# Conditioning products on VectorE, float32r biases and gates before the combine in a two-block diffusion transformer on one core

## The chip, the cores and the metric

The kernel runs on one NeuronCore of a Trainium2 chip. TensorE (PE) multiplies matrices into PSUM, VectorE (DVE) and ScalarE (ACT) work on SBUF and PSUM, GpSimd (POOL) helps, and SyncE (SP) issues nearly all DMA transfers of weights. The metric is device time in microseconds (us), the median of several runs. A profiled execution gives a span and a trace; its own time is a little longer than its span.

## What is computed

A batch of one: 256 tokens and 256 context tokens of width 1024 go through two transformer blocks, all in float32. Cut to what matters here:

```python
silu_c = jax.nn.silu(c)                                   # block 1; block 2 has its own c_2
mod = split(silu_c @ w_mod + b_mod, 6)                    # 6 vectors of 1024, from a 1024 x 6144 matrix
h = rmsnorm(x, norm_mix_g) * (1 + mod[1]) + mod[0]
x = x + mod[2] * token_mixer(h, h_ctx, ...)               # HGRN2 scans, latent attention, projections
h = rmsnorm(x, norm_ffn_g) * (1 + mod[4]) + mod[3]
x = x + mod[5] * moe_ffn(h, ...)                          # 32 experts, 4 for each token
    # per expert: gu = xb @ w_gate_up[e] + b_gate_up[e];  act = glu(gu);  y = act @ w_down[e] + b_down[e]
x = rmsnorm(x, final_norm_g)
x = second_block(x, c_2, ...)   # silu(c_2) @ w_ada + b_ada, RWKV7 and RG-LRU branches, a MoE of 4 x 8 experts
shf, scf = split(silu(c_2) @ w_ada_f + b_ada_f, 2)        # final norm: rmsnorm(x) * (1 + scf) + shf
```

The vectors `mod`, their counterparts of block 2 and `shf`, `scf` are called conditioning vectors below. The first 2048 columns of `w_mod` are needed at once and computed at the start by `mod_first`, which the change leaves alone.

## The kernel before

There are four stages: block 1 (0 to 576 us), its MoE (to 1540), block 2 (to 1842) and its MoE (to 2109).

**The queue of block 1.** Work on TensorE comes as Items: `prep` requests weights (1 MB tiles in a ring of five buffers), `run` is a generator that issues the products. `step` (L451) runs the first Item of the queue and prepares the first two, so weights are requested two Items ahead. Between the pieces of the HGRN2 scans, `fill` takes Items from the queue. A projection Item splits its weights in two float32r parts, `wsh` on ScalarE (L495) and the remainder `wsl` on VectorE (L496), and multiplies three times (L508 to L510, tile `tp`). All engines run their instructions in the order in which the program issues them.

**Conditioning products.** `mod(which, j)` (L371) is an Item with two 1 MB tiles: 512 of the outputs as a row, from 8 float32 products per tile pair (`modrow`, L367, into `modps`), added into the table `rowall` on VectorE (L369). `cpad` holds the silu of the conditioning so that a product writes one row. The list `MODS1` has 20 of them; `mixed` puts one behind each projection Item of block 1. The last four (`wadaf`) are loaded and run at the start of block 2. `mod_cols` later turns rows into columns, and `bcast_rows` (L425) broadcasts a row over all partitions by one product of 512 columns.

**The MoE of block 1** (`moe1`, `expert1a`, `expert1b`). For each expert 12 tiles of 1 MB come in. `expert1a` multiplies the 64 gathered tokens' columns with 8 of them into `gu` (L1327; two 64-row halves, two column halves), adds the bias by four products of 32 x 64 with rows of `brows` (L1402), and VectorE and ScalarE make the activation. `expert1b`, delayed by one expert, multiplies with the other four into `y` (L1358) and adds two bias products. `combine` (L1240) splits `y` times the slot weight into `yhi` (ScalarE, L1236) and `ylo` (VectorE, L1237), scatters with products `co` (L1248), and on VectorE four times multiplies by the gate vector (`gated`, L1253) and adds into `x` (L1254). Every four experts, tokens are gathered anew (`ga`, L1278). After expert 11 (`OVF`) the pending down product runs at once, expert 12's weights are requested into named buffers, and a branch for overfull experts is read (L1292).

**The start of block 2.** The four `wadaf` Items are put in the queue, two of them loaded ahead, then one tile of the projection weights. x is normalised (`xh`, L1672 and L1682), transposed on TensorE (`xT`, L1710), mixed (`hp`, `xm`), and projected.

Of the kernel before, what the change touches and what calls it, by code (L numbers as in the profile page):

```python
# [23 lines left out]
MODS1 = [(1, j) for j in range(4, 12)] + [(2, j) for j in range(12)]  # L24
NWS, NU, NV = 8, 32, 20
NWR = 5
# [5 lines left out]
def _cols(a):  # L32
# [23 lines left out]
def _khalf(w):  # L56

    t = w.shape[1] // 512
    return np.ascontiguousarray(w.reshape(2, 4, 128, t, 512).transpose(3, 0, 2, 1, 4)).reshape(2 * t, 128, 2048)
# [62 lines left out]
def layout(i):  # L122
# [12 lines left out]
    d['wmod'] = _khalf(i['w_mod'][0])  # L135
    d['wmix'] = _ktile(i['w_mod'][0][:, :2048])
    d['wada'] = _khalf(i['w_ada_2'][0])
    d['wadaf'] = _khalf(i['w_ada_f_2'])
    mix = i['b_mod'][0][:2048].reshape(2, 4, 256).transpose(1, 0, 2).reshape(-1)
    d['bmods'] = np.ascontiguousarray(np.concatenate([mix, i['b_mod'][0][2048:], i['b_ada_2'][0], i['b_ada_f_2'], mix]).reshape(32, 512))  # L140
# [36 lines left out]
class Item:  # L177

    def __init__(self, prep, run):
        self.prep, self.run = prep, run  # L180
        self.ready = self.done = False
        self.gen = self.then = None
# [57 lines left out]
class Ker:  # L240
    def __init__(self, tc, d, out, dbg=None, stop=None, start=1):
        self.tc, self.nc, self.d, self.out = tc, tc.nc, d, out
        self.dbg = dbg or {}
        self.stop, self.start = stop, start
# [5 lines left out]
    def run(self):  # L250
        with ExitStack() as es:
# [10 lines left out]
            if self.start <= 1:  # L262
                with tc.tile_pool(name="t1late", bufs=1, side="right") as pl, tc.tile_pool(name="t1", bufs=1) as p:
                    self.early = lambda n: p.tile([128, 512], F32, name=n, tag="u", bufs=NU)
                    self.consts()
                    route = self.block1(p, pl, xtile)
            else:
                self.early = lambda n: self.cp.tile([128, 512], F32, name=n)
                self.consts()
                self.x1 = xtile("x").rearrange("p a (b n) -> p (a b n)", b=1).rearrange("p (b n) -> p b n", b=2)  # L270
                self.nc.sync.dma_start(self.x1, self.d['xin'])
                self.add(*(self.mod(2, j) for j in range(12)))
                self.drain()
                self.mod_cols((12, 10, self.mcol2[:, 0:40]))
# [4 lines left out]
            if self.start > 1:  # L279
                self.load_gf()  # L280
            if self.start <= 1:
                with tc.tile_pool(name="moe1", bufs=1, side="right", reuse_waits="tile") as p, tc.tile_pool(name="w2", bufs=NW2, reuse_waits="tile") as wp2, tc.tile_pool(name="w2x", bufs=NW2X, reuse_waits="tile") as wp3:
                    self.wq = own * NWR + [(wp3, "w")] * NW2X + [(wp2, "w")] * NW2
                    self.moe1(p, route, (wp2, "w"), (wp3, "w"))
# [29 lines left out]
    def consts(self):  # L314
# [23 lines left out]
        self.cpad2 = cp.tile([128, 504], F32, name="cpad2").rearrange("p (k n) -> p k n", k=8)  # L338
        nc.gpsimd.memset(self.cpad2, 0.0)
        nc.gpsimd.tensor_copy(self.cpad2[:, :, 31], cs[:, 16:24])  # L340
# [6 lines left out]
        self.mcol2 = cp.tile([128, 48], F32, name="mcol2")  # L347

# [4 lines left out]
    def msrc(self, which, j):  # L353
        src, r = {1: ('wmod', j), 2: ('wada', 12 + j), 3: ('wadaf', 24 + j)}[which]
        return [self.d[src][2 * j + a] for a in range(2)], r
# [57 lines left out]
    def mod_cols(self, *todo):  # L413

        pt = self.fold_rows()
        for r, n, dst in todo:
            self.nc.vector.tensor_copy(dst.rearrange("p (j g) -> p g j", g=4), pt.rearrange("p (g r) -> p g r", g=4)[:, :, r:r + n])

    def bcast_rows(self, keys, dst, last=None):

        nc = self.nc
        for key, o in zip(keys, dst):
            ps = self.ps("bc")
            r = self.msrc(*key)[1]
            nc.tensor.matmul(ps, self.fold[:, r:r + 1].to_broadcast([128, 128]), self.rowall, start=True, stop=True)  # L425
            (last or nc.scalar.copy)(o, ps)
# [8 lines left out]
    def add(self, *items):  # L435
        self.q += items
        return items[-1]
# [99 lines left out]
    def block1(self, p, late, xtile):  # L537
# [255 lines left out]

        mods = [self.mod(*m) for m in MODS1]
        def mixed(items):
            out = []
            for it in items:
                out.append(it)
                if mods:
                    out.append(mods.pop(0))  # L800
# [66 lines left out]
        for pr in range(4):  # L867
# [4 lines left out]
            else:  # L872
                nxt = None
                lnexp()
                for i in range(3):
                    self.later(4 * i, lambda i=i: readout(i))
                self.add(*(tproj(win[28 + a], LAT, keep(qa, "qa", 3, qnorm)) for a in range(3)),
                         tproj(win[31], HS, keep(ckv, "ckv", 2, cnorm)), tproj(d['wrope'], HS, keep(kr, "kr"), nb=1, n=1024))
# [1352 lines left out]
```

## Time and profile before

| | us |
|---|---|
| runs, median (lowest to highest of 3) | 2112.69 (2109.07 to 2114.51) |
| the profiled execution, own time | 2111.07 |
| its span | 2109.3 |
| TensorE busy, in the span | 1945.5 (92%) |
| VectorE busy | 896.0 (42%) |
| ScalarE busy | 511.6 (24%) |

Busy shares are means over four stages with different limits, so the table by stretch and the slices of the span say more than they do. Matmuls are pipelined, and a busy TensorE is not one at its peak. A wait is put down to what came last; idle time of an engine that does not set the end costs nothing.

### The profile page before, as it was taken

How to read it: one execution, taken by the hardware profiler on the slowest of the kernel's cores; microseconds unless marked ns; L12 is line 12 of the kernel's file. 1: busy time of each engine (PE TensorE's matmuls, PEld its weight loads, DVE VectorE, ACT ScalarE, POOL GpSimd, SP SyncE). 2: the span in 40 equal slices, each digit the busy share in tenths (PEclk: the TensorE clock that was granted, in tenths of full speed). 3: DMA queues.
4: the chain of work that ended last, by engine and by line, in shares of the span. 5: the costliest groups of instructions: out<-in, count | busy, mean ns of one | idle time of the engine just before them, and what ended most of it. 6: DMA issues, size and time to landing. Idle time of an engine off the chain costs nothing. (4 is left out here: it accounts for less than half of the span.)

```text
span 2109.3 us, 30791 instructions
## 1 busy us (share of the span) xinstructions
PE 1945.5 (92%) x12860; PEld 1114.6 (53%) x12861; DVE 896.0 (42%) x1727; ACT 511.6 (24%) x893; POOL 63.3 (3%) x66
## 2 busy tenths in 40 slices
PE   5999999999899999989999999999969998899785
PEld 3888788877733333333333333333338997764331
DVE  5666754445423233332323333242378574421112
ACT  3433454344300001000000100000035543311011
POOL 0000000000000000000000000000032201000000
PEclk9999999999999999989999999999989999989897
DMA  9255636732699999979999999999873133289895
GB/s 362 81 219 201 227 126 258 278 111 80 262 415 427 411 427 416 427 295 407 426 427 427 426 427 427 426 427 427 365 292 124 62 121 103 114 370 420 360 425 226
DMA packets 95272, 646.11 MB, mean 306 GB/s; under 512 B 11668, under 2 KB 12692, under 8 KB 19220
## 3 DMA queue, kind: packets, MB, share of 16 engines
q1 hardware_dynamic: 93296, 642.79, 74.9%
q8 instruction: 104, 1.70, 0.3%
q10 hardware_dynamic: 1828, 1.26, 0.2%
q14 instruction: 44, 0.36, 0.0%
HBM read 642.96 MB, written 1.05 MB: 305 GB/s over the span
## 5 line engine op out<-in xcount | busy, mean ns | idle before, releaser
L1327 PE MATMUL gu<-w,gT 128*64 128x512 f32 x2048 | 481.2, 597 | 0.0
L1327 PEld LDWEIGHTS gu<-w,gT 128*64 128x64 f32 x2048 | 148.1, 137 | 278.1 <-issue 263.1
L1358 PE MATMUL y<-w,aT 128*64 128x512 f32 x1024 | 229.4, 601 | 0.4
L496 DVE TENSOR_TENSOR wsl<-w,wsh 128x1024 fp32r<-128x1024 f32 (+1 forms) x141 | 168.6, 1205 | 97.6 <-ACT wsh L495 97.3
L495 ACT CAST wsh<-w 128x1024 fp32r<-128x1024 f32 (+1 forms) x141 | 143.4, 1030 | 169.0 <-PE tp L509 97.4
L1337 DVE TENSOR_SCALAR act<-gu 128x256 f32<-128x256 f32 x64 | 27.2, 425 | 307.5 <-PE gu L1402 304.2
L1237 DVE SCALAR_TENSOR_TENSOR ylo<-y,sw,yhi 128x512 fp32r<-128x512 f32 x52 | 39.0, 751 | 264.5 <-ACT yhi L1236 264.0
L1358 PEld LDWEIGHTS y<-w,aT 128*64 128x64 f32 x1024 | 71.9, 139 | 148.6 <-issue 143.7
L508 PE MATMUL tp<-hs,wsh 128*128 128x256 f32 (+1 forms) x424 | 139.7, 329 | 0.0
L510 PE MATMUL tp<-hs,wsl 128*128 128x256 f32 (+1 forms) x424 | 134.3, 317 | 4.1 <-DVE wsl L496 4.1
L509 PE MATMUL tp<-hs,wsh 128*128 128x256 f32 (+1 forms) x424 | 133.6, 315 | 0.0
L1529 PE MATMUL ab<-w,gT 128*32 128x256 f32 (+1 forms) x1024 | 99.8, 415 | 17.4 <-DMA w<-in_w1e_dram 10.8
L1236 ACT ACTIVATE yhi<-y,sw 128x512 fp32r<-128x512 f32 x52 | 35.8, 688 | 300.9 <-PE y L1402 239.9
L1253 DVE TENSOR_TENSOR gated<-co,gtb 128x512 f32<-128x512 f32 x128 | 88.3, 690 | 34.6 <-PE co L1248 27.5
L1339 ACT ACTIVATE sge<-act 128x512 f32<-128x512 f32 x32 | 20.1, 630 | 331.3 <-DVE act L1337 331.3
L508 PEld LDWEIGHTS tp<-hs,wsh 128*128 128x128 f32 x424 | 81.7, 193 | 16.3 <-issue 4.9
L1254 DVE TENSOR_TENSOR x<-x,gated 128x512 f32<-128x512 f32 x128 | 88.3, 690 | 3.3
L510 PEld LDWEIGHTS tp<-hs,wsl 128*128 128x128 f32 x424 | 81.6, 193 | 9.9 <-DVE wsl L496 4.9
L508 PE MATMUL tp<-hi,wsh 128*128 128x256 f32 x288 | 85.4, 296 | 0.0
L509 PEld LDWEIGHTS tp<-hs,wsh 128*128 128x128 f32 x424 | 81.8, 193 | 4.5 <-issue 0.7
L1278 PE MATMUL ga<-oh,xhi 128*128 128x256 f32 x208 | 63.5, 333 | 21.9 <-PEq L1292 6.3
L509 PE MATMUL tp<-lo,wsh 128*128 128x256 f32 x288 | 81.7, 284 | 0.0
(576 smaller groups left out, 3099.9 us busy)
## 6 DMA issues: line engine op xcount, KB each, us to landing
w<-in_wgu_dram SPq DMA_DIRECT2D x256, 1024.0 KB, 15.3
w<-in_wdn_dram SPq DMA_DIRECT2D x128, 1024.0 KB, 15.6
w<-in_win_dram SPq DMA_DIRECT2D x50, 1024.0 KB, 5.9
w<-in_w3e_dram SPq DMA_DIRECT2D x32, 1024.0 KB, 14.7
w<-in_w1e_dram SPq DMA_DIRECT2D x32, 1024.0 KB, 11.9
w<-in_w2e_dram SPq DMA_DIRECT2D x32, 1024.0 KB, 15.9
w<-in_wada_dram SPq DMA_DIRECT2D x24, 1024.0 KB, 6.4
w<-in_wmod_dram SPq DMA_DIRECT2D x16, 1024.0 KB, 6.0
```

The costliest lines, as they stand in the source:

```text
L495: nc.scalar.copy(hi, src)
L496: nc.vector.tensor_sub(lo, src, hi.bitcast(F32))
L508: nc.tensor.matmul(out, a[0], b[0], start=first, stop=False)
L509: nc.tensor.matmul(out, a[0], b[1], start=False, stop=False)
L510: nc.tensor.matmul(out, a[1], b[0], start=False, stop=last)
L1237: nc.vector.scalar_tensor_tensor(lo, y, w, hi.bitcast(F32), op0=OP.mult, op1=OP.subtract)
L1253: nc.vector.tensor_mul(part, o[s], gate[:, cs])
L1254: nc.vector.tensor_add(x[:, b, cs], x[:, b, cs], part)
L1278: nc.tensor.matmul(ps[:, 256 * kk:256 * kk + 64 * n], xs[i][:, b, 128 * (k + kk):128 * (k + kk) + 128], ohv[b], start=(b + i == 0), stop=( ...
L1327: nc.tensor.matmul(gu[j][64 * s:64 * s + 64, :], g[:, k, c0:c0 + 64], w[:, 1024 * s + 512 * j:1024 * s + 512 * j + 512], start=(k == 0), s ...
L1358: nc.tensor.matmul(y[64 * s:64 * s + 64, :], aT[:, k % 4, k // 4, :], w[:, o:o + 512], start=(k == 0), stop=False)
L1529: nc.tensor.matmul(ps[m * j:m * j + m, 256 * i:256 * i + 256], g[:, k, c0 + m * j:c0 + m * j + m], w[j][:, k, :], start=(k == 0), stop=(k ...
```

## The change

**Conditioning products on VectorE.** The host transposes `w_mod`, `w_ada` and `w_ada_f` so that outputs lie on partitions. `crow` broadcasts the silu of the conditioning over 128 partitions (eight products and two copies, once for c and once for c_2). An Item is now half a former one, with one 1 MB tile and two `scalar_tensor_tensor` instructions of 128x1024 with an accumulator; a bias add of 128x2 follows. The result is a column of `mcol1`, `mcol2` or `mcol3`. Halves are `light`: `step` prepares them when it meets them and counts only other Items to two. All 24, the four `wadaf` too, run in block 1: one half behind each projection of the scans, one behind each of the latent projections, two behind the gates `g7` and the query projections, the rest behind the last key/value Item.

**Biases.** Bias rows are split once into float32r parts, high and low on 64 partitions for each half, and an expert adds them with one selection matrix (`brow`, made on VectorE, 128x128) and three products: two into `gu`, one into `y`.

**Gates.** `expert1b` multiplies `y` by the gate once (128x512) before the split; `combine` then adds `co` from PSUM into `x` directly.

**Block 2** starts without conditioning products; its first projection tile is requested first.

```diff
-MODS1 = [(1, j) for j in range(4, 12)] + [(2, j) for j in range(12)]
+MODS = [(1, j) for j in range(4, 12)] + [(2, j) for j in range(12)] + [(3, j) for j in range(4)]
...
     def step(self):
         it = self.q[0]
-        for i in self.q[:2]:
+        n = 0
+        for i in self.q:
             if not i.ready:
                 i.ready, i.w = True, i.prep()
+            n += not i.light
+            if n == 2:
+                break
...
-    def mod(self, which, j):
-        src, r = self.msrc(which, j)
-        cpad = self.cpad1 if which == 1 else self.cpad2
-        def run(ws):
-            yield from self.modrow(cpad, r, [(0, lambda k: ws[k // 4][:, 512 * (k % 4):512 * (k % 4) + 512])])
-        return Item(lambda: [self.wload(t) for t in src], run)
+    def mod(self, p, which, j):
...
+        def half(a):
+            def run(w):
+                yield 0
...
+                for i in range(2):
+                    wi = w[:, 1024 * i:1024 * i + 1024]
+                    n = 2 * a + i
+                    nc.vector.scalar_tensor_tensor(wi, wi, 1.0, c, op0=OP.mult, op1=OP.mult, accum_out=o[:, n:n + 1])
+                o = o[:, 2 * a:2 * a + 2]
+                b = VOFF[bias] + 4 * j + 2 * a
+                nc.vector.tensor_add(o, o, self.vec[:, b:b + 2])
+            return Item(lambda: self.wload(self.d[src][2 * j + a]), run, True)
+        return [half(0), half(1)]
...
-        lastg = [self.add(tproj(win[24 + i], LAT, g7)) for i in range(4)][-1]
+        lastg = [self.add(*mixed([tproj(win[24 + i], LAT, g7)], 2)) for i in range(4)][-1]
...
         for j in range(2):
-            for s in range(2):
-                bias(gu[j][64 * s:64 * s + 64, :], 0, 1024 * s + 512 * j)
+            bias(gu[j], 0, 512 * j)
...
-        for s in range(2):
-            bias(y[64 * s:64 * s + 64, :], 1, 512 * s)
-        self.combine(p, x, y, oT, wv, gate)
+        bias(y, 1, 0)
+        part = p.tile([128, 512], F32, name="gated", tag="gated", bufs=1)
+        nc.vector.tensor_mul(part, y, gate)
+        self.combine(p, x, part, oT, wv)
...
-        mods = [self.mod(3, j) for j in range(4)]
-        self.add(*mods)
-        for m in mods[:2]:
-            m.ready, m.w = True, m.prep()
         ahead = [(self.wload(win2[2]),)]
```

What this moves on VectorE shows in block 1 between the latent keys and the softmax. Before, around the gate projections (`wsl` is a projection's weight remainder, `sg` and `s` the gate's sigmoid, `rowall` the add of a conditioning product):

```order
L369 TENSOR_TENSOR rowall<-rowall,modps 128x512
L496 TENSOR_TENSOR wsl<-w,wsh 128x1024 x2
L864 TENSOR_TENSOR sg<-sg,tp 128x512
L865 TENSOR_TENSOR s_3680<-s_3680,sg 128x512
L369 TENSOR_TENSOR rowall<-rowall,modps 128x512
L496 TENSOR_TENSOR wsl<-w,wsh 128x1024 x9
L496 TENSOR_TENSOR wsl<-w,wsh 128x512
L496 TENSOR_TENSOR wsl<-w,wsh 128x1024
```

And now, in the same place, around the projections of `g7` and the queries (`mcol` is a conditioning column, `crow` the broadcast silu):

```order
L507 TENSOR_TENSOR wsl<-w,wsh 128x1024 x2
L386 SCALAR_TENSOR_TENSOR w,mcol_97<-w,crow 128x1024 x2
L389 TENSOR_TENSOR mcol_97<-mcol_97,vec 128x2
L386 SCALAR_TENSOR_TENSOR w,mcol_97<-w,crow 128x1024 x2
L389 TENSOR_TENSOR mcol_97<-mcol_97,vec 128x2
L507 TENSOR_TENSOR wsl<-w,wsh 128x1024 x2
L386 SCALAR_TENSOR_TENSOR w,mcol_97<-w,crow 128x1024 x2
L389 TENSOR_TENSOR mcol_97<-mcol_97,vec 128x2
L386 SCALAR_TENSOR_TENSOR w,mcol_97<-w,crow 128x1024 x2
L389 TENSOR_TENSOR mcol_97<-mcol_97,vec 128x2
L507 TENSOR_TENSOR wsl<-w,wsh 128x1024
L507 TENSOR_TENSOR wsl<-w,wsh 128x512
```

Four full-width instructions stand between one Item's remainders and the next one's, where one add stood or none. From the latent keys' normalisation to the ninth softmax reduction the order has 64 of them; in front of it 32: 14 up to the first scan pair's readout copy, 11 in the second pair, 7 in the third.

In the MoE of block 1, VectorE's instructions behind an expert's down product were:

```order
L1237 SCALAR_TENSOR_TENSOR ylo<-y,sw,yhi 128x512
L1253 TENSOR_TENSOR gated<-co,gtb_5348 128x512
L1254 TENSOR_TENSOR x<-x,gated 128x512
L1253 TENSOR_TENSOR gated<-co,gtb_5348 128x512
L1254 TENSOR_TENSOR x<-x,gated 128x512
L1253 TENSOR_TENSOR gated<-co,gtb_5348 128x512
L1254 TENSOR_TENSOR x<-x,gated 128x512
L1253 TENSOR_TENSOR gated<-co,gtb_5348 128x512
L1264 CAST oT<-wT 128x256
L1254 TENSOR_TENSOR x<-x,gated 128x512
```

They are now (`blk` and `fc` make the selection matrix of the next bias):

```order
L1376 TENSOR_TENSOR gated<-y,gtb_5348 128x512
L1438 TENSOR_SCALAR brow<-blk,fc 128x128
L1251 SCALAR_TENSOR_TENSOR ylo<-gated,sw,yhi 128x512
L1270 TENSOR_TENSOR x<-x,co 128x512 x4
L1280 CAST oT<-wT 128x256
```

One product by the gate stands before the split instead of four behind the scatter.

## Rows read from the trace of the kernel before

**Rows 1.** The page: span, busy time of engines, and GB/s in 40 slices.

```profile
span 2109.3 us, 30791 instructions
...
PE 1945.5 (92%) x12860; PEld 1114.6 (53%) x12861; DVE 896.0 (42%) x1727; ACT 511.6 (24%) x893; POOL 63.3 (3%) x66
...
GB/s 362 81 219 201 227 126 258 278 111 80 262 415 427 411 427 416 427 295 407 426 427 427 426 427 427 426 427 427 365 292 124 62 121 103 114 370 420 360 425 226
```

**Rows 2.** Stretches: from:to, length, busy us (instructions) by engine, clock, DMA share, GB/s.

```profile
64.00:143.00 79.00, 75.50 (x504) 64.67 (x503) 56.91 (x135) 34.92 (x71) 0.00 (x0) 0.96 0.47 174
143.00:211.00 68.00, 68.00 (x469) 56.65 (x468) 39.95 (x99) 26.91 (x58) 0.00 (x0) 1.00 0.49 186
211.00:271.00 60.00, 60.00 (x403) 48.61 (x402) 39.38 (x99) 26.05 (x58) 0.00 (x0) 1.00 0.57 211
...
322.00:489.00 167.00, 162.02 (x1152) 130.72 (x1150) 78.78 (x116) 69.13 (x104) 0.00 (x0) 1.00 0.58 211
...
950.00:1400.00 450.00, 438.58 (x2196) 154.92 (x2193) 147.28 (x261) 35.72 (x58) 0.00 (x0) 1.00 1.01 424
1537.00:1570.00 33.00, 17.23 (x109) 7.54 (x109) 25.63 (x39) 13.12 (x26) 14.15 (x16) 0.74 0.77 292
```

**Rows 3.** Stretches, instructions on the tile modps alone: PE, PEld, DVE busy.

```profile
64.00:143.00 79.00, 5.98 (x48) 1.15 (x48) 2.05 (x3) 0.96 0.47 174
143.00:211.00 68.00, 7.90 (x64) 1.57 (x64) 2.73 (x4) 1.00 0.49 186
...
322.00:425.00 103.00, 15.39 (x128) 3.34 (x128) 5.47 (x8) 1.00 0.73 273
```

**Rows 4.** Groups by line, VectorE, 64 to 322: count, busy us, mean ns.

```profile
L369 DVE TENSOR_TENSOR rowall<-rowall,modps 128x512 f32<-128x512 f32 x12 | 8.2, 684 | 2.0 <-PE modps L367 1.9
...
L680 DVE MEMSET ex<- 128x1 f32 x7 | 0.4, 59 | 0.0
```

**Rows 5.** Two lines, whole trace: duration ns min/median/max, first and last start.

```profile
L1138 DVE SCALAR_TENSOR_TENSOR xlo<-x,rs,xhi x4: 1276/1278/1279, 569.1 to 1838.7; 128x1024 fp32r<-128x1024 f32 x4
...
L957 ACT ACTIVATION_READ_ACCUMULATOR pr<-sc,st x16: 191/192/195, 440.2 to 523.3; 128x1 f32 x16
```

**Rows 6.** Groups by line, VectorE, 1537 to 1570: busy us, mean ns.

```profile
L1253 DVE TENSOR_TENSOR gated<-co,gtb 128x512 f32<-128x512 f32 x4 | 2.8, 690 | 0.7 <-PE co L1248 0.6
...
L1237 DVE SCALAR_TENSOR_TENSOR ylo<-y,sw,yhi 128x512 fp32r<-128x512 f32 x1 | 0.8, 751 | 6.6 <-ACT yhi L1236 6.6
L1676 DVE SCALAR_TENSOR_TENSOR tn<-tn,tn 128x1 f32<-128x1 f32 x2 | 0.3, 155 | 0.1
```

**Rows 7.** TensorE's waits, 322 to 489: us in total, times, longest.

```profile
PE tp L510 <- DVE wsl L496: 4.1, 3, 1.6
```

**Rows 8.** Timeline after expert 11: start, us, engine, instruction [idle before <-releaser].

```profile
905.50 1.93 PE L1402 MATMUL gu<-brows,fc 32*64 32x512 f32 x8
...
914.38 1.07 PE L1402 MATMUL y<-brows,fc 32*64 32x512 f32 x4
...
939.68 0.55 PE L1278 MATMUL ga<-oh,xhi 128*128 128x256 f32 x1 [6.23 <-DVEq L1292]
...
933.02 0.69 DVE L1253 TENSOR_TENSOR gated<-co,gtb 128x512 f32<-128x512 f32 x1 [0.58 <-PE co L1248]
...
914.49 14.08 SPq L311 DMA_DIRECT2D w<-in_wgu_dram  x8
```

**Rows 9.** Timeline of TensorE at the start of block 2.

```profile
1556.76 0.87 PE L1710 MATMUL xT<-fc,xh 128*128 128x128 f32 x3 [14.71 <-DVE xh L1682]
...
1561.60 2.56 PE L367 MATMUL modps<-w,cpad 128*32 128x512 f32 x16
...
1565.30 1.93 PE L367 MATMUL modps<-w,cpad 128*32 128x512 f32 x16
...
1569.11 0.28 PE L508 MATMUL tp<-hi,wsh 128*128 128x256 f32 x1
1569.23 0.28 PE L509 MATMUL tp<-lo,wsh 128*128 128x256 f32 x1
```

More of the change, by code (lines that the diff above doesn't have):

```diff
@@ L261, in run @@
             self.last_sig = None
[L262 to L268, printed above, removed]
-                self.consts()
[L270 to L274, printed above, removed]
+            with tc.tile_pool(name="t1late", bufs=1, side="right") as pl, tc.tile_pool(name="t1", bufs=1) as p:
+                self.early = lambda n: p.tile([128, 512], F32, name=n, tag="u", bufs=NU)
+                self.consts()
+                route = self.block1(p, pl, xtile)
             if self.stop == 1:
@@ L278, in run @@
             self.gf = self.rp.tile([128, 1024], F32, name="gf", tag="gf")
[L279 to L284, printed above, removed]
+            with tc.tile_pool(name="moe1", bufs=1, side="right", reuse_waits="tile") as p, tc.tile_pool(name="w2", bufs=NW2, reuse_waits="tile") as wp2, tc.tile_pool(name="w2x", bufs=NW2X, reuse_waits="tile") as wp3:
+                self.wq = own * NWR + [(wp3, "w")] * NW2X + [(wp2, "w")] * NW2
+                self.moe1(p, route, (wp2, "w"), (wp3, "w"))
             if self.stop == 2:
@@ L351, in v, with mcol @@
         return self.vec[:, o:o + 1]
-    def msrc(self, which, j):
-        src, r = {1: ('wmod', j), 2: ('wada', 12 + j), 3: ('wadaf', 24 + j)}[which]
-        return [self.d[src][2 * j + a] for a in range(2)], r
+    def mcol(self, which, j):
+        return {1: self.mcol1[:, 0, :], 2: self.mcol2, 3: self.mcol3}[which][:, 4 * j:4 * j + 4]
     def modrow(self, cpad, r, pieces):
@@ L423, in bcast_rows @@
             ps = self.ps("bc")
-            r = self.msrc(*key)[1]
-            nc.tensor.matmul(ps, self.fold[:, r:r + 1].to_broadcast([128, 128]), self.rowall, start=True, stop=True)
+            for g in range(4):
+                nc.tensor.matmul(ps[:, 128 * g:128 * g + 128], self.mcol(*key)[:, g:g + 1].to_broadcast([128, 128]), self.ident, start=True, stop=True)
             (last or nc.scalar.copy)(o, ps)
@@ L436, in add @@
         self.q += items
-        return items[-1]
+        return items[-1] if items else None
     def later(self, us, fn):
@@ L792, in block1, with mixed @@
                 s.forget(i, b, pf[i][b])
-        mods = [self.mod(*m) for m in MODS1]
-        def mixed(items):
+        self.crows = None, None
+        mods = [h for m in MODS for h in self.mod(p, *m)]
+        def mixed(items, n=1):
             out = []
@@ L876, in block1 @@
                     self.later(4 * i, lambda i=i: readout(i))
-                self.add(*(tproj(win[28 + a], LAT, keep(qa, "qa", 3, qnorm)) for a in range(3)),
-                         tproj(win[31], HS, keep(ckv, "ckv", 2, cnorm)), tproj(d['wrope'], HS, keep(kr, "kr"), nb=1, n=1024))
+                self.add(*mixed([*(tproj(win[28 + a], LAT, keep(qa, "qa", 3, qnorm)) for a in range(3)),
+                                 tproj(win[31], HS, keep(ckv, "ckv", 2, cnorm)), tproj(d['wrope'], HS, keep(kr, "kr"), nb=1, n=1024)]))
                 est = 10.3 + 30.7
@@ L1238, in weighted, with combine @@
         return hi, lo
-    def combine(self, p, x, y, oT, w, gate, bufs=1):
+    def combine(self, p, x, y, oT, w, gate=None, bufs=1):
         nc = self.nc
@@ L1251, in combine @@
                 cs = slice(512 * s, 512 * s + 512)
-                part = p.tile([128, 512], F32, name="gated", tag="gated", bufs=1)
-                nc.vector.tensor_mul(part, o[s], gate[:, cs])
+                part = o[s]
+                if gate is not None:
+                    part = p.tile([128, 512], F32, name="gated", tag="gated", bufs=1)
+                    nc.vector.tensor_mul(part, o[s], gate[:, cs])
                 nc.vector.tensor_add(x[:, b, cs], x[:, b, cs], part)
@@ L1396, in wl, with bias_of @@
             return lambda j: first.pop((e, j)) if isinstance(e, int) and (e, j) in first else fetch(e, j)
-        def bias_of(pick):
+        def bias_of(one):
+            rows = p.tile([128, 128], F32R, name="brow", tag="brow", bufs=2)
+            nc.vector.tensor_scalar(rows, blk, one, None, op0=OP.mult)
             def bias(o, which, c):
-                j, c = (2, c) if which else divmod(c, 1024)
-                r = slice(32 * j, 32 * j + 32)
-                nc.tensor.matmul(o, pick(r, j).to_broadcast([32, 64]), brows[r, c:c + 512], start=False, stop=True)
+                bias_parts()
+                nc.tensor.matmul(o, rows, brow[which][:, c:c + 512], start=False, stop=True)
             return bias
         def late(g, c0, i, ohv, w):
-            bsel = p.tile([96, 1], F32, name="bsel")
-            for j in range(3):
-                r = slice(32 * j, 32 * j + 32)
-                nc.vector.tensor_copy(bsel[r, :], self.ident[r, 32 * j:32 * j + 32][:, bass.ds(i, 1)])
-            bias = bias_of(lambda r, j: bsel[r, 0:1])
+            bsel = p.tile([128, 1], F32, name="bsel")
+            nc.vector.tensor_copy(bsel, self.fold[:, bass.ds(i, 1)])
+            bias = bias_of(bsel)
             self.expert1b(p, x, self.expert1a(p, g, c0, wl(i), bias), wl(i), bias, ohv, w, gtb)
```

92 lines of the change are left out of this document (61 added, 31 removed), and 3 rows, old and new, of the table VECS.

## The prediction

> **What bounds the kernel now.** I read the page first: its engine line and the slices [rows 1]. The profiled execution took 2111.07 us, 1.8 us more than its span; the median of the runs is 2112.69, so a sum made against 2111.07 stands 1.6 us below what is quoted. TensorE (PE) is busy 92% of the span and VectorE (DVE) 42%, but that is an average over stages with different limits. The slice rows separate them (I count slices of 52.7 us from 0): from slice 11 to 27 (580 to 1476 us, most of the first MoE) the transfers move 407 to 427 GB/s in every slice but slice 17 (295); in slices 1 to 10 they move 80 to 278.
>
> The table by stretch confirms it [rows 2]. In block 1 TensorE is busy 68.00 of 68 and 60.00 of 60 us: it is the bound, and VectorE has a third of the time free or more. From 322 to 489 VectorE is busy only 78.78 of 167. From 950 to 1400 the DMA share is 1.01 at 424 GB/s while TensorE is busy 438.58 of 450: the weight stream bounds and TensorE follows just behind. From 1537 to 1570 nothing is full.
>
> **1. Conditioning products.** The 20 that stand in block 1 cost TensorE 39.3 us by their tile's rows, 16 instructions and 1.97 us each: 5.98 us for three of them up to 143, 7.90 for four in each of the next two stretches, one more up to 322, and 15.39 for eight after it [rows 3]. All of it is in stretches where TensorE is full, so all of it could come back, if VectorE can carry what replaces it. VectorE loses 20 adds of 0.684 us [rows 4] and gets 24 products (the four of the final norm come forward) of four `scalar_tensor_tensor` 128x1024 with an accumulator, and two bias adds. The nearest instruction, two f32 operands of 128x1024 from SBUF, takes 1.278 us; the accumulator has no VectorE row. On ScalarE its read is an instruction of its own, 0.192 us [rows 5], and VectorE's shortest instruction is 0.059 us [rows 4]. So one accumulating instruction costs between 1.28 and 1.47; I take 1.34, the short end, since VectorE's own small instructions are short. A bias add is 0.16, as the 128x1 one [rows 6].
>
> Where they stand decides. By the order, 14 stand in the first pair of scans (64 to 143), 11 in the second, 7 in the third, none before the latent keys (ckv), then 64 in what before was 322 to 489.
> - 64 to 143: VectorE 56.91 - 2.05 + 14 x 1.34 + 7 x 0.16 = 74.7; TensorE 75.50 - 5.98 = 69.5. VectorE now needs most, and it also has waits of its own, so the 79 us stay: gain 0 (-4 to 4).
> - 143 to 211: VectorE 39.95 - 2.7 + 14.7 + 0.9 = 52.9; TensorE 60.1. TensorE stays the bound: gain 6 of 7.9 (3 to 8), less for in-order waits.
> - 211 to 271: 46.6 against 52.1: gain 7 of 7.9 (5 to 8). 271 to 322: one product less on a full TensorE, gain 2.
> - 322 to 489: VectorE 78.78 - 5.47 + 64 x 1.34 + 32 x 0.16 = 164.2; TensorE 162.02 - 15.39 and some 2 us to broadcast the conditioning row, 149. The bound changes hands. Before, TensorE waited for VectorE's weight remainders (`wsl`) 4.1 us in all here [rows 7]; now every one of them queues behind products of 2.7 us a pair. With 6 us of VectorE's waits for ScalarE and TensorE the stretch takes 170: loss 3 (loss 15 with 1.47 and longer waits, gain 10 if part of the 64 slips into the softmax behind).
>
> The new halves take no place among the two items that are prepared ahead, so the projections' weights are still requested two items early; bytes are the same. Rows are broadcast by four products of 128 columns instead of one of 512, the same columns: 0. Block 1 together: 0 + 6 + 7 + 2 - 3 = 12 (-12 to 30).
>
> **2. Biases of the first MoE.** An expert pays 1.93 us after the gate/up products and 1.07 after the down product [rows 8], 3.0 together. Three fp32r products replace them. Products of that kind with 256 columns start 0.12 us apart [rows 9], so 0.24 each for 512 and 0.7 per expert: TensorE saves 2.3 per expert, 74 us over 32. That is not time: the stream bounds. What it can give is the stream's pauses. Slices 11, 13 and 15 move 415, 411 and 416 against 427 [rows 1], that is (12 + 16 + 11)/427 x 52.7 = 4.8 us; with buffers freed earlier I take 3 (0 to 5). The small products `brow` (128x128) lie on VectorE, which is busy a third there. The twelve small bias transfers instead of three are requested on SyncE among weights that are long ahead of use: 0.
>
> **3. The gap after expert 11.** Slice 17 lacks (427 - 295)/427 x 52.7 = 16 us of stream [rows 1]. The requests that fill expert 12's buffers start at 914.49 on SyncE, as the delayed down product of expert 10 ends (its bias starts at 914.38); in front of it lies expert 11's gate/up bias, 1.93 us that become 0.5: 1.4 earlier. TensorE also comes into the gap earlier, having had up to 4 x 2.3 less work in the group; I take 3. Then expert 12's gather waits 6.23 us, to 939.68, for VectorE's eight combine instructions, of which the first starts at 933.02 [rows 8]. Four of them go: 4 x 0.69 = 2.8 [rows 6], and 2 x 0.8 of down biases, less 0.7 for the new gate product in front of ScalarE's `yhi`: 3.7. Together 8 (4 to 14).
>
> **4. The end of the first MoE.** After the last tiles land, TensorE has the biases of expert 31 and of expert 30's down product (1.93 + 2 x 1.07 become 0.9: 3.2 less), and the last combine four products less (2.8, of which some 2 are on the path, since the adds wait for TensorE in turn), less 0.7 for the gate: 4 (3 to 6).
>
> **5. Start of block 2.** Four products stood here. Two run before the transposes, in front of an idle time of 14.71 that VectorE ends, and cost nothing; two stand on TensorE's path between the transposes and the first projections, 2.56 and 1.93 us [rows 9]: 4.5. Two adds of 0.68 ahead of the normalisation go from VectorE, and the projection weights are no longer requested behind 8 MB of conditioning weights. I take 6 (3 to 12).
>
> **Sum.** The rest of block 2 and its MoE do not change. 12 + 3 + 8 + 4 + 6 = 33: 2111.07 - 33 = **2078 us**, 1.6% less. Bounds of the terms taken together go from 2111 - 67 to 2111 + 2, but ends rarely meet.
>
> **Rivals.**
> A. VectorE has room after all: its instructions are independent, and TensorE's queue hides their lateness. Then all 39 us of block 1 come back, less 2 for the broadcast, and 21 of the rest: 2053. For it: VectorE is busy half to three quarters of block 1 [rows 2]. Against: 164 against 149 in 322 to 489.
>
> B. The accumulating instruction is dear, and the kernel gets slower. Place: 322 to 489, where 64 stand. With s us for one, VectorE needs 78.4 + 64 s there and 55.9 + 14 s in the first pair, and some 10 us of waits: block 1 changes by 78 s - 102 - 15, the rest by -21. That is no gain at s = 1.8, and from there each 0.1 us costs 8. If each element took twice as long, s would be 1.278 + 2 x 0.527 = 2.33 (0.527 is what 512 elements more cost, 1.278 against 0.751 [rows 5, 6]): block 1 grows by 65, the total is 2155. Against: xlo, with two f32 operands from SBUF, runs at full rate; but it has no accumulator, so it can't exclude this. [...]
>
> C. Block 1 gives nothing and the gap neither: the halves hold places in the ring of five weight buffers until VectorE reaches them, so the projections' tiles are requested late, and the stream resumes no sooner. Left are terms 4 and 5: 2101.
>
> D. The first MoE is really bound by TensorE (97% busy from 950 to 1400 [rows 2]), and the 74 us come back: with terms 1, 4 and 5 near 2015. Against: a DMA share of 1.01.
>
> **How the numbers follow.** The forecast 0.61, A 0.14, C 0.14, B 0.09, D 0.02. The range 2050 to 2108 takes the forecast's case whole, most of C and half of A, and leaves out B, D and ends of both: 2 in 10. About 0.3% (6 us) is what a measurement can tell from no change. Faster: 0.61 + 0.14 + 0.02 + 0.08 of C = 0.85; within: 0.06, mostly C; slower: 0.09, B.
>
> **What would show it.** The accumulating instructions at 1.28 to 1.47 us (above 1.8: B). From the latent keys to the softmax VectorE nearly full, and TensorE waiting for `wsl` some 20 us instead of 4.1 (A if it doesn't). The first scan pair unchanged, the next two 6 to 7 us shorter. The stream still at 424 GB/s with TensorE less busy (D if the rate rises no further and the stage shortens with TensorE), slice 17's pause halved. No products between the transposes and the first projection of block 2. The forecast is wrong if the projections wait for their weights in block 1, or if the gap after expert 11 stays.

## The result and the profile after

The changed kernel takes 2056.14 us, median of four runs (2055.9 to 2057.89), against 2112.83 of the kernel before (2109.07 to 2114.51) beside it: ratio 0.9736, 95% interval 0.9719 to 0.9753. The time is inside the forecast range, but the gain is 56.7 us and not 33. The profiled execution took 2057.89 us, 53.2 less than the one of before, and the table below accounts for these 53.2.

The page of the kernel after (as [rows 1]: span, TensorE, VectorE, moved GB/s in 40 slices of 51.4 us):

```profile
span 2056.1 us, 29718 instructions
...
PE 1848.4 (90%) x12284; PEld 1116.6 (54%) x12285; DVE 927.5 (45%) x1886; ACT 514.9 (25%) x899; POOL 61.3 (3%) x64
...
GB/s 370 85 232 191 141 103 349 329 288 97 363 419 419 419 420 419 420 380 420 420 419 419 420 420 419 419 419 419 410 180 88 64 125 123 131 385 419 365 420 229
```

TensorE lost 97 us of busy time, VectorE gained 31. Two things in the last row were not in the forecast: the pause in slice 17 has almost gone (295 to 380), and every full slice of the first MoE stands at 419 or 420 GB/s where before it stood at 427 [rows 1].

Stretches of the kernel after (as [rows 2]): the three pairs of scans, the latent keys to the softmax, and 450 us of the first MoE:

```profile
64.00:146.50 82.50, 78.97 (x532) 73.14 (x531) 71.42 (x165) 39.23 (x77) 0.00 (x0) 0.96 0.46 162
146.50:200.00 53.50, 53.48 (x353) 48.61 (x352) 50.95 (x128) 26.29 (x58) 0.00 (x0) 1.00 0.57 205
200.00:253.30 53.30, 53.30 (x354) 48.91 (x353) 45.07 (x115) 26.87 (x58) 0.00 (x0) 1.00 0.43 147
...
299.70:463.00 163.30, 153.57 (x1045) 132.53 (x1043) 149.55 (x278) 70.80 (x110) 0.00 (x0) 0.97 0.84 311
...
890.00:1340.00 450.00, 414.56 (x2040) 158.90 (x2042) 117.78 (x232) 37.09 (x60) 0.00 (x0) 0.99 1.00 415
```

The second and third pair are still full on TensorE and much shorter. In the fourth row neither engine is full: TensorE idles 9.7 us and VectorE 13.8. In the last row TensorE is busy 414.56 us where it was 438.58 [rows 2].

Stage marks in us, from the traces (start of the latent keys' scaling, of the ninth softmax reduction, of the first gate/up product of experts 0, 11, 12 and 31, of block 2's first transposition, of its MoE's first product, and the end):

| kernel | latent keys | softmax | exp. 0 | exp. 11 | exp. 12 | exp. 31 | xT | MoE 2 | end |
|---|---|---|---|---|---|---|---|---|---|
| before | 321.7 | 490.2 | 576.0 | 887.9 | 943.4 | 1492.7 | 1556.8 | 1842.5 | 2109.3 |
| after | 299.7 | 463.1 | 546.2 | 843.9 | 898.3 | 1448.3 | 1509.0 | 1793.2 | 2056.1 |
| conditioning alone | 299.5 | 463.0 | 546.2 | 858.9 | 914.4 | 1466.9 | 1532.7 | 1819.7 | 2083.6 |
| biases and gate alone | 323.0 | 491.4 | 576.1 | 875.6 | 929.0 | 1465.7 | 1523.3 | 1821.5 | 2085.0 |
| after, 224 bytes more | 299.9 | 463.7 | 546.9 | 844.5 | 898.1 | 1434.6 | 1495.4 | 1779.8 | 2040.9 |
| the same, halves spread | 298.9 | 447.9 | 529.4 | 828.0 | 880.3 | 1417.5 | 1477.4 | 1761.5 | 2022.5 |

Of the 53.2 us, block 1 gave 29.8 (22.0 up to the latent keys, 5.1 to the softmax, 2.7 to expert 0), experts 0 to 11 gave 14.2, the gap 1.1, experts 12 to 31 lost 0.7, the end of the MoE gave 3.4, block 2 up to its MoE 1.5 and the rest 3.9.

### The profile page after: what moved, and what is told of

It reads as the page before. It is cut to its first block, busy times and chain, and to the rows that moved or that the text cites. A ratio compares the mean times of both kernels' runs of the same rounds, so it can differ in the third digit from the quotient of the medians.

```text
span 2056.1 us, 29718 instructions
## 1 busy us (share of the span) xinstructions
PE 1848.4 (90%) x12284; PEld 1116.6 (54%) x12285; DVE 927.5 (45%) x1886; ACT 514.9 (25%) x899; POOL 61.3 (3%) x64
## 5 line engine op out<-in xcount | busy, mean ns | idle before, releaser
L1343 PEld LDWEIGHTS gu<-w,gT 128*64 128x64 f32 x2048 | 157.5, 137 | 260.1 <-issue 231.5
L1373 PE MATMUL y<-w,aT 128*64 128x512 f32 x1024 | 234.8, 602 | 15.1 <-DMA w<-in_wdn_dram 14.1
L386 DVE SCALAR_TENSOR_TENSOR w<-w,crow 128x1024 f32<-128x1024 f32 x96 | 115.4, 1220 | 2.0 <-DMA w<-in_wmod_dram 2.0
L1567 PE MATMUL ab<-w,gT 128*32 128x256 f32 (+1 forms) x1024 | 95.6, 404 | 15.5 <-DMA w<-in_w1e_dram 8.8
L1376 DVE TENSOR_TENSOR gated<-y,gtb 128x512 f32<-128x512 f32 x32 | 22.1, 692 | 183.7 <-PE y L1442 183.7
L1270 DVE TENSOR_TENSOR x<-x,co 128x512 f32<-128x512 f32 x128 | 79.4, 682 | 19.1 <-PE co L1262 19.1
L521 PEld LDWEIGHTS tp<-hs,wsl 128*128 128x128 f32 x424 | 82.5, 195 | 6.2 <-DVE wsl L507 1.2
L1250 ACT ACTIVATE yhi<-gated,sw 128x512 fp32r<-128x512 f32 x32 | 23.1, 721 | 250.3 <-DVE gated L1376 250.3
```

Source lines behind the costliest of these rows:

```text
L386: nc.vector.scalar_tensor_tensor(wi, wi, 1.0, c, op0=OP.mult, op1=OP.mult, accum_out=o[:, n:n + 1])
L521: nc.tensor.matmul(out, a[1], b[0], start=False, stop=last)
L1270: nc.vector.tensor_add(x[:, b, cs], x[:, b, cs], part)
L1343: nc.tensor.matmul(gu[j][64 * s:64 * s + 64, :], g[:, k, c0:c0 + 64], w[:, 1024 * s + 512 * j:1024 * s + 512 * j + 512], start=(k == 0), s ...
L1373: nc.tensor.matmul(y[64 * s:64 * s + 64, :], aT[:, k % 4, k // 4, :], w[:, o:o + 512], start=(k == 0), stop=False)
L1567: nc.tensor.matmul(ps[m * j:m * j + m, 256 * i:256 * i + 256], g[:, k, c0 + m * j:c0 + m * j + m], w[j][:, k, :], start=(k == 0), stop=(k ...
```

## Experiments

**The same kernel again.** Kernel before, unchanged, as a control of the traces: one run.

> The kernel before once more, for its stream of expert weights beside the runs of this job. In the trace of before the stream of the first MoE ran at 424 GB/s from 950 to 1400 (slices of 426 and 427), in the trace of the changed kernel at 419 in every slice. Theory 1: the rate belongs to the kernel (in the changed kernel SyncE waits for transfers, 374 of 450 us, and hardly for TensorE, so the queue is always full): here 424 to 427 again, and 419 in the next kernels where biases and gates are changed. Theory 2: the rate belongs to the chip or the execution: here the same rate as in the other kernels of this job.

It took 2109.32 us. Its marks lie within 1.7 us of the first profile's, and its stream (GB/s in 40 slices, as above) shows the same level:

```profile
GB/s 362 81 221 200 229 123 260 277 111 80 263 417 427 413 427 413 427 294 407 427 427 426 427 427 427 427 427 426 371 291 122 65 121 102 110 369 421 369 424 227
```

So 427 against 419 belongs to the kernel, and not to one execution.

**Conditioning alone.** The kernel after with the biases and the gate of before.

```
-        bias(y, 1, 0)
-        part = p.tile([128, 512], F32, name="gated", tag="gated", bufs=1)
-        nc.vector.tensor_mul(part, y, gate)
-        self.combine(p, x, part, oT, wv)
+        for s in range(2):
+            bias(y[64 * s:64 * s + 64, :], 1, 512 * s)
+        self.combine(p, x, y, oT, wv, gate)
```

> Only the conditioning products are moved; biases and gates as before. Theory 1 (the parts add up by stage): block 1 ends 27 to 30 us earlier, block 2's start gains 5 to 6, the first MoE nothing: 2112.8 - 34 = 2079. Rival: earlier weights or fewer waits in block 1 also help the first MoE, or the first MoE takes back part since its first weights arrive later relative to TensorE: 2065 or 2090.

Measured 2084.16 (ratio 0.9872, 0.9855 to 0.9888). Block 1 keeps all of the 29.8 us, and what follows it keeps nothing more (expert 0 to the end 1537.4 us, before 1533.3). The stream is the slower one here too, with the old biases: 412 GB/s over experts 0 to 11, where before moved 415.

**Biases and gate alone.** The kernel before with the new biases, `blk` and gated rows.

```
-        for s in range(2):
-            bias(y[64 * s:64 * s + 64, :], 1, 512 * s)
-        self.combine(p, x, y, oT, wv, gate)
+        bias(y, 1, 0)
+        part = p.tile([128, 512], F32, name="gated", tag="gated", bufs=1)
+        nc.vector.tensor_mul(part, y, gate)
+        self.combine(p, x, part, oT, wv)
```

> Only biases and gates of the first MoE are changed; conditioning products as before, the weight buffers at a multiple of 256 bytes. Theory (TensorE's saving lets the stream run without pauses, at 427): the first MoE gains its pauses (5 us), 10 us at the gap after expert 11 and 3 to 4 behind the last expert: 2112 - 19 = 2093. Rival (bound by TensorE): 2043. Rival (the gain hangs on the conditioning part): 2108.

Measured 2086.73 (ratio 0.9895, 0.9879 to 0.9912). The table shows the parts: experts 0 to 11 give 12.4 us and 12 to 31 give 12.6, together with the gap 27, the MoE's end gives 6.5, and then block 2 loses 12.5 (xT to its MoE 298.2 against 285.7). With the four final conditioning products still at block 2's start, SyncE requests in this order (start, duration; `win` are block 2's projection weights, first transposition at 1523.31):

```profile
1501.82 0.33 SPq L311 DMA_DIRECT2D w<-in_wadaf_dram  x1
1503.53 0.33 SPq L311 DMA_DIRECT2D w<-in_win_dram  x1
1513.21 10.56 SPq L311 DMA_DIRECT2D w<-in_wadaf_dram  x4
1526.41 32.91 SPq L311 DMA_DIRECT2D w<-in_win_dram  x7
...
1547.85 0.39 PE L508 MATMUL tp<-hi,wsh 128*128 128x256 f32 x1
```

The first projection starts 24.5 us after the transposition; before it was 11.8, after 4.8. All of its weights but one are requested 3 us after the transposition or later; after, five were requested 14 us or more ahead of it. So the four products that the other half moves away from block 2's start cost more behind a shorter MoE. Alone the halves give 27 and 21 us against the kernel before beside each, together 57 (65 where the weight buffers start as before, see below).

**Old gate.** The kernel after with the gate applied to `co`, four products, as before.

```
-        part = p.tile([128, 512], F32, name="gated", tag="gated", bufs=1)
-        nc.vector.tensor_mul(part, y, gate)
-        self.combine(p, x, part, oT, wv)
+        self.combine(p, x, y, oT, wv, gate)
```

> The changed kernel with the gates as before: four products by the gate behind the scatter, none in front of the split. Theory: the stream hides it for 30 experts; it shows at the gap after expert 11 and behind the last expert, 2 us each: 2056 + 4 = 2060. Rival (the extra product in front of the split costs at every expert, as waits of the scatter for ScalarE's yhi grew from 0.8 to 1.6 us): 2056 or below.

Measured 2064.77 (ratio 0.9777, 0.9759 to 0.9795), 8.6 us above the kernel after. The gate on `y` is worth that much, but spread: experts 0 to 11 2.1, end of the MoE 1.6, block 2's start 1.8, and 1.2 even in block 1, which the edit does not touch and which shows the scatter of such marks. The gap after expert 11, where 2 us were expected, is 1.8 shorter (52.6 against 54.4).

**Where the weight buffers lie.** The change takes `cpad2` (504 columns) out of the constants and adds 16 columns of `mcol3` and 112 of `vec`. All buffers behind them move down by 1504 bytes. In the kernel before, the weight buffers start at a multiple of 256 bytes; after, 32 bytes beyond one. Two kernels tell what that does: the kernel after with 224 unused bytes, and the kernel before shifted by 32.

```
-        self.mcol3 = cp.tile([128, 16], F32, name="mcol3")
+        self.mcol3 = cp.tile([128, 72], F32, name="mcol3")
```

> The changed kernel with 224 unused bytes per partition more in the constants, so that the weight buffers start again at a multiple of 256 bytes, as in the kernel before (in the changed kernel they start 32 bytes behind one). Nothing else differs. Theory (the start address of the buffers sets the stream's rate): 427 GB/s in the first MoE instead of 419, 0.5 us per expert and 12 to 16 us in all: 2056 - 13 = 2043. Rival (the rate belongs to something else in the conditioning part, such as the layout of its weights): 419 again and 2056.

```
-        self.mcol2 = cp.tile([128, 48], F32, name="mcol2")
+        self.mcol2 = cp.tile([128, 56], F32, name="mcol2")
```

> The kernel before with 32 unused bytes more in its constants, so that its weight buffers start 32 bytes behind a multiple of 256. Nothing else differs. Theory: 419 instead of 427 GB/s, the experts' stream 0.5 us longer for each of 32, partly in pauses that it has anyway: 2111 + 10 = 2121. Rival (the address doesn't matter): 2111.

The pages, GB/s in 40 slices, first the kernel after with 224 bytes more, then the shifted kernel before:

```profile
GB/s 374 84 224 194 137 99 346 330 288 99 352 426 426 427 427 426 427 383 426 427 426 427 426 427 426 426 427 426 394 176 91 64 123 124 132 386 424 366 425 230
```

```profile
GB/s 362 81 221 199 231 122 259 277 111 80 270 412 419 411 420 419 419 310 408 419 420 419 419 420 419 419 420 419 416 303 108 76 109 117 104 385 419 368 420 223
```

The start address alone moves the stream from 427 to 419 and back. It costs the kernel after 13.6 us by the medians, 10 by the ratios (2042.52 without it; ratio to before 0.9687, 0.9671 to 0.9703), nearly all of it between experts 12 and 31 by the marks: 550.0 us against 536.5. The kernel before loses little by it (2110.46; ratio 1.0009, 0.9998 to 1.0020; between experts 12 and 31 of its trace 3.0 us). That settles what bounded its first MoE: a slower stream by 1.8% over 900 us would have cost 16 us if the stream alone had been the bound. It was TensorE as well. SyncE's waits say the same (us, times, longest), before from 943.4 to 1492.7:

```profile
SPq L311 <- PE gu L1327: 199.7, 106, 14.2
SPq L311 <- DMA w<-in_wgu_dram: 128.4, 82, 2.6
SPq L311 <- DMA w<-in_wdn_dram: 72.3, 42, 2.3
SPq L311 <- PE y L1358: 48.4, 36, 4.3
```

and after from 898.3 to 1448.3, where SyncE waits for the transfers almost alone:

```profile
SPq L300 <- DMA w<-in_wgu_dram: 301.6, 142, 4.6
SPq L300 <- DMA w<-in_wdn_dram: 145.6, 70, 2.2
SPq L300 <- PE gu L1343: 8.8, 11, 6.2
```

In the first, half of the time a request waits for TensorE to give a buffer back: the two share the bound. In the second the stream alone is late.

How 32 bytes cost 1.8% no run shows: the page tells of what is read, and here the rows that are written are displaced. Nor do the runs show that 256 is the step that counts; for the buffers of the first MoE they have starts at a multiple of it and 32 bytes beyond one.

**The expert weights of block 2 too.** As the first edit, and `shb` longer by 24 columns, so that block 2's second pool starts at a multiple of 256 bytes.

> As the aligned kernel, and 96 bytes more in front of the eight buffers of the second MoE, which start 160 bytes behind a multiple of 256 in the kernel before (192 in the changed one) and then at one. Theory: its stream moves 427 instead of 420 where it is full, 96 tiles, 3 to 4 us less: 2039. Rival: the second MoE is set by TensorE and by its start, no difference to the aligned kernel.

Measured 2041.43 (ratio 0.9677, 0.9661 to 0.9694): not to be told from 2042.52. That stage isn't bound by its stream throughout, or the pool is too small a part; this wasn't followed further.

**VectorE's share in block 1: shorter products.** The kernel after, each accumulating product over 256 of its 1024 columns (three quarters of every sum are left out, so later stages see other numbers).

```
-                    nc.vector.scalar_tensor_tensor(wi, wi, 1.0, c, ...
+                    nc.vector.scalar_tensor_tensor(wi[:, :256], wi[:, :256], 1.0, c[:, :256], ...
```

> The changed kernel with each accumulating product over 256 of the 1024 columns; the other three quarters of every sum are left out, so the conditioning vectors are not the reference's. VectorE loses some 80 us of work in block 1, nothing else changes. Theory 1 (VectorE is not the bound, except in the first pair of scans; what TensorE still loses after the latent keys are waits for ScalarE's casts at the ends of items): 3 to 4 us in the first pair, 2 to 3 after the latent keys, 2050. Theory 2 (VectorE is the bound from the latent keys to the softmax, as forecast): that stretch falls from 163 to TensorE's 154, with the first pair 13 to 14 us, 2042.

One run, 2054.08. Latent keys to softmax, the stretch and TensorE's largest waits in it:

```profile
299.20:454.10 154.90, 148.45 (x1045) 129.06 (x1044) 101.96 (x278) 70.76 (x110) 0.00 (x0) 1.00 0.88 335
...
PE tp L519 <- ACT wsh L506: 4.7, 2, 3.0
PE kn L519 <- ACT wsh L506: 1.6, 1, 1.6
```

(`tp` are projections, `kn` keys.) The stretch takes 8.5 us less, block 1 in all 9.2; the first pair of scans gives 1.5 of it at most (its readout copy at 145.0, after 146.5). But the run changes more than the length: with other lengths the instructions also come in another order. Behind the gates' sigmoids at 361.19, 366.95 and 372.71 the kernel after has two, no and two casts on ScalarE; here they are two, one and one. So the 8.5 us are of length and order together. With VectorE busy only 102 of 155 us TensorE still waits 6.3 us, and for ScalarE's casts (`wsh`): that part isn't VectorE's. Of the 9.2 us at most 4 show in the total of this one run; why later stages took longer stays open.

**VectorE's share: double products.** The kernel after, each product issued a second time, with ones.

```
+                    nc.vector.scalar_tensor_tensor(wi, wi, 1.0, self.ones[:, 0:1].to_broadcast([128, 1024]), ...
```

> The changed kernel with each accumulating product done twice (the first by a constant one, into the same place). Theory (one costs VectorE 1.14 us from start to start, its accumulator read lies under the next instruction): after the latent keys VectorE needs 150 + 64 x 1.14 = 223 and some 8 of waits, 231 instead of 163; the first pair 87 + 6 instead of 82, the second 65 instead of 53, the third 54; together 80 to 90 us, 2140. With the price of the forecast (1.34) it is 105 to 115, 2165. Rival (VectorE still has room, the products are hidden): under 40, 2095.

One run, 2114.39, 58 us more than the kernel after. Latent keys to softmax:

```profile
313.90:521.90 208.00, 174.39 (x1090) 146.94 (x1088) 202.94 (x375) 69.57 (x109) 0.00 (x0) 0.91 0.65 227
```

VectorE is busy 202.94 of 208: here it is the bound. The stretch holds 115 products instead of 64 (the rest has moved out of it); 51 more at 1.14 us are 58, and it grew by 44.6, since 13.8 us of VectorE had been free. I had expected 80 to 90 us in all, each product paid in full; in the scan pairs VectorE's free time took part of them as well.

**Halves spread.** The kernel after with 224 bytes more, one half behind each gate and query projection instead of two, and the nine pairs that are left behind attention steps.

```
-        lastg = [self.add(*mixed([tproj(win[24 + i], LAT, g7)], 2)) for i in range(4)][-1]
+        lastg = [self.add(*mixed([tproj(win[24 + i], LAT, g7)], 1)) for i in range(4)][-1]
...
-            self.add(*mixed([tproj(d['wqb'][i], QS, keep(qn, "qn"), nk=6, n=1536)], 2))
+            self.add(*mixed([tproj(d['wqb'][i], QS, keep(qn, "qn"), nk=6, n=1536)], 1))
```

> The aligned kernel with the halves spread wider: one behind each gate and query projection instead of two, and the nine that are left in pairs behind the attention steps, where VectorE is busy 39 of 83 us and the transfers move 190 GB/s. If VectorE is what binds from the latent keys to the softmax, that stretch falls from 163 to 156 or so and the attention keeps its 83: 2042.5 - 6 = 2036. If TensorE's waits there are for ScalarE's casts, the stretch stays and the attention grows by what the softmax's chain waits for VectorE, 2 to 4 us: 2045.

Measured 2025.9 us (2024.28 to 2028.3; ratio 0.9603, 0.9584 to 0.9622), the fastest version: 83 us below the kernel before, 17 below the one with 224 bytes more. Latent keys to softmax:

```profile
298.90:447.90 149.00, 148.93 (x1052) 129.76 (x1051) 142.01 (x263) 70.54 (x109) 0.00 (x0) 1.00 0.87 314
```

TensorE is busy 148.93 of 149 at full granted clock, although 59 of the 64 products still lie in this stretch and VectorE carries 142 us. So it was not mainly VectorE's length that cost with pairs. ScalarE and TensorE of the kernel after where one gate projection ends (`s` is the sigmoid, `wsh` the cast of the next Item's weights):

```profile
372.71 0.60 ACT L647 ACTIVATE s<-tp 128x512 f32<-128x512 f32 x1 [5.16 <-PE tp L521]
373.20 1.98 ACT L506 CAST wsh<-w 128x1024 fp32r<-128x1024 f32 x2
...
374.29 0.39 PE L519 MATMUL tp<-hs,wsh 128*128 128x256 f32 x1 [1.62 <-ACT wsh L506]
```

and ScalarE of the spread kernel at such an end:

```profile
366.11 1.05 ACT L506 CAST wsh<-w 128x1024 fp32r<-128x1024 f32 x1 [1.87 <-PE tp L520]
367.07 0.60 ACT L647 ACTIVATE s<-tp 128x512 f32<-128x512 f32 x1
368.95 1.05 ACT L506 CAST wsh<-w 128x1024 fp32r<-128x1024 f32 x1 [1.29 <-PE tp L520]
```

With pairs, both casts of the next projection stand behind the sigmoid at this end, which waits for TensorE's last product; TensorE then waits for the cast. Spread, the first cast stands ahead of the sigmoid and TensorE runs through: it has no wait in the whole stretch. In the kernel before, TensorE had a conditioning product there: one of 1.92 us starts at 331.90, and the sigmoid at 332.62 with its casts lies beside it. What the change took off TensorE had also been cover at this place.

## Why the prediction was right and where it failed

**Sign and range: right, the range in part by luck.** TensorE's products were paid where TensorE was full [rows 2, 3], and came back there. But the terms missed by 17.8 us (block 1), 10.5 (first MoE), -6.9 (the gap) and -1.2 (the rest), and a slower stream that no term had took 10 to 14 back. With the buffers at the old start the same change gives 2042.5, below the range of 2050 to 2108.

**The price of an accumulating instruction: this step failed.** I took 1.34 us, within 1.28 to 1.47, from durations [rows 5], and 0.16 for a bias add [rows 6]. The line's two groups after (duration min/median/max in ns), and a timeline of VectorE:

```profile
L386 DVE SCALAR_TENSOR_TENSOR w<-w,crow x96: 1205/1220/1236, 109.7 to 459.0; 128x1024 f32<-128x1024 f32 x96
L386 DVE DVE_READ_ACCUMULATOR w<-w,crow x96: 74/84/101, 110.9 to 460.1; 128x1 f32 x96
```

```profile
343.48 0.16 DVE L389 TENSOR_TENSOR mcol<-mcol,vec 128x2 f32<-128x2 f32 x1
343.55 1.23 DVE L386 SCALAR_TENSOR_TENSOR w<-w,crow 128x1024 f32<-128x1024 f32 x1
344.69 0.09 DVE L386 DVE_READ_ACCUMULATOR w<-w,crow 128x1 f32 x1
344.69 1.23 DVE L386 SCALAR_TENSOR_TENSOR w<-w,crow 128x1024 f32<-128x1024 f32 x1
```

The accumulator's read lies under the next instruction's start, and one product starts 1.14 us after the last though it lasts 1.22. The bias add is followed after 0.07. So a sum of durations is too high here: for the stretch after the latent keys I had 164.2 us of VectorE; it is busy 149.55. Rival B (2.33 us each) falls with it: these rows stand at 1.22, and no run shows the doubling it supposes.

**Block 1: forecast 12, measured 29.8.** The first pair gave -4.4 where I had 0; by the rows above it holds 28 more of TensorE's instructions than before (532 in 82.5 us, 504 in 79 [rows 2]) although 48 of its conditioning products are gone [rows 3]: 61 more are of the projections' tile `fp` and 16 make `crow` (1.95 us; the 2 in the forecast were an estimate without a row). So Items moved from pair to pair. The pairs and the way to the latent keys come to 22.0 together, where I had 15. The stretch to the softmax gave 5.1 where I had a loss of 3. There my reading of the wait was wrong. I had VectorE as the bound; TensorE waits for `wsl` 1.7 us, not some 20, and 7.9 for ScalarE's casts:

```profile
PE tp L519 <- ACT wsh L506: 6.3, 3, 3.0
PE kn L519 <- ACT wsh L506: 1.6, 1, 1.6
PE kn L521 <- DVE wsl L507: 0.9, 1, 0.9
PE tp L521 <- DVE wsl L507: 0.8, 1, 0.8
```

What holds it is shown by the spread halves: with 59 of the 64 products still there, at the same length, the whole 14.4 us are gone. It is where the products stand among remainders and casts. The shorter products took 8.5, but in another order too. Of the 14.4 some 10 are idle time, and 4.6 is TensorE's busy time (153.57 against 148.93), at the lower clock. Between 370 and 390 the granted clock is 0.83 on average, before and behind it 1.00. TensorE had idled 1.6 and 0.8 us, up to 374.3 and 375.6; 1 us later its products start 0.21 us apart instead of 0.12, and the granted clock is 0.50 from 377 to 379:

```profile
376.13 0.28 PE L519 MATMUL tp<-hs,wsh 128*128 128x256 f32 x1
376.25 0.28 PE L520 MATMUL tp<-hs,wsh 128*128 128x256 f32 x1
...
376.72 0.41 PE L520 MATMUL tp<-hs,wsh 128*128 128x256 f32 x1
376.93 0.42 PE L521 MATMUL tp<-hs,wsl 128*128 128x256 f32 x1
```

VectorE's in-order queue thus had the wrong price and the smaller part of the waits, and the handoff to ScalarE, the larger one, was missing from the sum.

**First MoE: forecast 3, measured 13.5.** "That is not time: the stream bounds" was wrong by half: TensorE bounded with it. A DMA share of 1.01 stands beside 424 GB/s before [rows 2] and 419 after; it does not exclude a second bound beside the stream. Before, the eighth gate/up tile of an expert up to expert 11 landed at least 16.6 us ahead of its use; after, that lead falls to 6.7 us at expert 7 and 1.3 at expert 11, and the stretch shrinks by 14.2 us, although the stream is slower. Without the shift of the buffers experts 12 to 31 give another 12.8; with it, nothing. So the term of the products is 27, of which the address took 13.6 back. No view of the trace of before shows the buffers' start; it follows from the sizes of what the kernel allocates ahead of them.

**The gap: forecast 8, measured 1.1 by TensorE's marks and 11 by the stream.** The rows that answer to [rows 8]:

```profile
862.31 0.73 PE L1442 MATMUL gu<-bra,brow 128*128 128x512 f32 x2
...
871.05 0.49 PE L1442 MATMUL y<-brb,brow 128*128 128x512 f32 x1
871.16 12.21 SPq L300 DMA_DIRECT2D w<-in_wgu_dram  x8
...
894.61 0.55 PE L1294 MATMUL ga<-oh,xhi 128*128 128x256 f32 x1 [6.36 <-DVE brow L1438]
```

The biases take 0.73 and 0.49 (1.93 and 1.07 before), and the requests start 8.9 us after expert 11's bias instead of 9.0. Expert 12's gather still waits 6.36 us (6.23 before). The reading of that wait failed: I put it down to VectorE's combine and took 3.7 us off. TensorE's own branch for overfull experts is as long. The view by that line of the program, before and after (in the queue of weight loads, ns min/median/max, first and last start in us):

```profile
L1292 PEldq COMPARE_BRANCH x2: 5908/6046/6185, 933.1 to 1962.6; - x2
L1308 PEldq COMPARE_BRANCH x2: 6003/6074/6145, 888.1 to 1910.7; - x2
```

VectorE's takes 0.07. Before, TensorE's branch ended at 939.01 and the combine at 939.00, so the combine alone could give nothing. After, the combine ends at 890.54, and `brow` and the gather wait for TensorE's branch, to 894.15. In the two traces these branches take 5.91 to 6.19 us. Why they do stays open.

The stream misses (419 - 380)/419 x 51.4 = 4.8 us in slice 17 instead of 16, because its lead had run out: expert 11's last tile lands at 879.1, after the new requests have begun (871.16), where before it landed at 906.4, 8 us ahead of them. So the pause was not shortened, as I had it, by earlier requests; the stream came to it later.

**End of the MoE and block 2: forecast 10, measured 8.8.** The end gave 3.4 (forecast 4). Block 2's first projection comes 7 us earlier after the transposition, as I had it (6):

```profile
1509.03 1.99 PE L1742 MATMUL xT<-fc,xh 128*128 128x128 f32 x8 [13.89 <-DVE xh L1715]
1511.88 2.06 PE L1742 MATMUL xT<-fc,xh 128*128 128x128 f32 x8 [0.85 <-ACT hi L1747]
1513.80 0.58 PE L519 MATMUL tp<-hi,wsh 128*128 128x256 f32 x1
```

Nothing of that is left at its 289th product (69.5 us after the transposition, before 68.8): TensorE's wait for `bh`, which VectorE makes, grew from 3.0 to 4.9 us. What else took it back was not followed. The other 3.9 come behind the start of block 2's MoE, where nothing was changed; over all traces this stage lies between 260.4 and 266.9 us, and the cause stays open.

**The rivals.** The time is near rival A's (2053), and only partly for its reason: block 1 gave 7 less than A has, because of the order on VectorE and ScalarE; with the halves spread it gives 46.6, more than A has. D was a third right: 27 of 74 us. C is out: ScalarE's casts waited 15.5 us for tiles of `win` up to expert 0 before, and 2.0 after.

## What to carry to other kernels

Price an instruction on VectorE by the distance of starts between two of its kind (here 1.14 us), not by its duration (1.22), and look at what else its neighbours hand on: here TensorE waited more for the cast behind the sigmoid than for VectorE. A wait that is put down to what came last can have a second cause that ends beside it, as TensorE's branch did. A full transfer queue does not say that it bounds alone: see for whom the requesting engine waits. And when a change alters the size of a constant, look at where the streamed buffers start; 224 unused bytes were worth 10 to 14 us.

## What was unexpected of the hardware

- Rows of the weight buffers that start 32 bytes beyond a multiple of 256 move at 419 or 420 GB/s in the full slices of the first MoE in after and in the shifted before; before, its repetition and after with 224 bytes more, which don't have it, stand at 426 or 427.
- `scalar_tensor_tensor` of 128x1024 with two f32 operands and an accumulator takes 1.22 us, starts 1.14 apart, and its accumulator's read (0.084) costs no time between two of them.
- Two idle times of 1.6 and 0.8 us at 374 and 375, and again one of 3.0 up to 385.8, were followed by a fall of TensorE's clock (0.50 from 377 to 379, 0.59 from 386 to 390), and the stretch was busy 4.6 us longer than with the halves spread. With shorter products one idle time of 3.0 was not: the clock is 1.00 over the whole stretch, 299.2 to 454.1.
- TensorE's branch takes 5.91 to 6.19 us in the traces of before and after, VectorE's 0.07.
